# One decoder layer on one core: side work priced by measured durations, the memory norm in pieces, the norm's sums spread out, a final norm from two banks

## The chip, the cores and the metric

The kernel runs on one core of one Trainium2 chip. The metric is the device time of one execution in microseconds, the median of three runs. A core has five engines that matter here: PE (TensorE, matrix products), DVE (VectorE), ACT (ScalarE), POOL (GpSimd) and SP, which only issues transfers. Each engine works through its own queue in order and waits for the others by semaphores. PE writes its results into PSUM banks, from which DVE and ACT read.

## The reference

One layer of a hybrid decoder for a prompt of 256 tokens and 8 sample tokens (264 columns in all), width 2048, in float32:

```python
def layer(x, ...):
    z = rmsnorm(x, g_mix) @ w_in                      # all group inputs from one projection
    # group 1: causal conv, gates, RG-LRU recurrence, gelu, norm   -> y_rg (1024 wide)
    # group 2: mLSTM, 4 heads, key width 128, value width 256
    h_ml, C_new, n_new, m_new = mlstm(q, k, v, logi, logf, C0, n0, m0)
    h_ml = rmsnorm(h_ml, g_ml_out)                    # per head
    y_ml = h_ml * sigmoid(z[..., OFF_O:OFF_I])
    x = x + concatenate([y_rg, y_ml]) @ w_out
    # cross attention: 4 heads over 256 memory tokens; the prompt's keys and values are computed,
    # those of the 8 samples are read from a cache
    x = x + softmax(xq @ mk.T * scale) @ mv @ w_xa_o  # mk, mv = rmsnorm(mem, g_mem) @ w_k, w_v
    xf = rmsnorm(x, g_ffn)
    x = x + (silu(xf @ w_ffn_gate) * (xf @ w_ffn_up)) @ w_ffn_down
# y = rmsnorm(x, g_final)
```

For the 8 sample tokens the mLSTM is one step of the recurrence: C_new = dec * C + k v, num = q . C_new, for each of 4 heads and 8 samples a state of 128 x 256.

## The kernel before, in words

**Weight blocks.** All products with weights are cut into 257 blocks: w_in is blocks 0 to 40, w_out 41 to 56, w_q 57 to 72, w_k and w_v 73 to 104, w_o 105 to 120, the FFN 121 to 256, the last 16 of which are the last part of the down projection. A block gives 128 rows of an output of 264 columns. Its weight of 2048 x 128 comes as two halves (tile `raw`), and each half is split into a high and a low part (tile `W`: high by an ACT copy to fp32r, low by a DVE subtraction). PE computes hi*hi + hi*lo + lo*hi, 48 matmuls of 128x264 a block, 24 a half. `W` has four half buffers, so half k can be written once PE has finished half k-2 blocks. Blocks are counted here in half steps: W of 33.5 is the second half of block 33. The result stands in a PSUM bank `mm`, of which there are four, and is read by an evacuation on DVE (`t<-mm,rstd` or `xres<-xres,mm`). Other products use four banks `ax`.

**Side work** (norms, gates, the mLSTM, attention) is written as Python generators. `side(g, prio)` registers one, and after each block `pump` lets them run, in order of priority, until a price model of DVE and ACT (`price_dve`, `price_act`, `price_pe`, an estimate in us for each instruction) has reached the end of the block by the model of PE; `yield STEP` ends a generator's turn for this block, and a generator of negative priority always runs. `later(f, after=n)` and `drip` put small PE jobs between the weight matmuls, n chunks of them apart. Afterwards a scheduler with a timeline of its own sets the order on each engine; SP's queue is written out by hand. Nearly every instruction passes through one helper, line 63, so in the profile groups are told apart by their tiles.

**The mLSTM's side work** lies in blocks 20 to 40. `ml_prompt` computes for each head h the masked, decayed scores `Pm` (DVE: `B<-ax,gcol`, then two `mask`, then `B<-ax,B 128x384`, with exponentials on ACT between them). `ml_heads` then gives PE the numerators `nps` and the new state `cps` of that head. `ml_sample` works on the sample states: POOL fetches a chunk of four states (`B<-c0T`) and their keys and queries, broadcast to all partitions (`B<-scr`), ACT makes the products k v (`t<-B,B`, two a state), DVE updates the state (`B<-B,bcs,t`, 128x256) and takes its product with q (`t<-B,B` with a sum output that an instruction of its own, DVE_READ_ACCUMULATOR, reads out, two a state). `ml_norm` takes sums of squares over partitions by one-column matmuls with `ones` (`acc_rg` is the like for the other group), makes the norm's factors `f` and spreads them over partitions.

**The memory norm** (`mem_gen`) computes 16 chunks of squares, then their norm, then scales each chunk (POOL, line 998) and splits it into high and low for w_k and w_v.

**The tail.** The squares of the final x are added up in `acc_x`; the sum over partitions is made by one-column matmuls with `ones`, those of the first 15 chunks inside the last block and those of the last chunk behind it (`fin_sums`). `rstd_fin` makes the factor, spreads it (`ax<-ident,c`) and copies it to `rstd` on ACT; DVE multiplies 12 of the 16 chunks of y from the bank, POOL four (chunks 4, 5, 10, 11) from `rstd`, and SP writes `o_y`.

Of the kernel before, what the change touches and what calls it, by code (L numbers as in the profile page):

```python
# [11 lines left out]
F32R = mybir.dt.float32r  # L12
# [5 lines left out]
P = 128  # L18
# [4 lines left out]
N = T + NS  # L23
# [43 lines left out]
def price_dve(name, n, a, k):  # L67
    fast = name in ("tensor_scalar", "tensor_copy", "tensor_single_scalar", "memset")
    if name == "tensor_reduce":
        n = int(np.prod(a[1].shape[1:]))  # L70
    return 0.07 + n * (0.00052 if fast else 0.0066 if name == "reciprocal" else 0.00104)


def price_act(name, n, a, k):
    return 0.12 + n * 0.00083


def price_pe(name, n, a, k):
    passes = 1 if name == "transpose" or a[1].dtype == F32R else 4
    return passes * n * 0.00042 + 0.003  # L80


@with_exitstack
def layer_kernel(ctx: ExitStack, tc, xT, memT, vec, wrg, w_in, w_out, w_q, w_k, w_v, w_o,
# [302 lines left out]
    def rstd_fin(ps):  # L387
        v, r, t = ctile(3), ctile(3), ctile(3)
        dve.tensor_scalar(v, ps[:, :3], 1.0 / D, EPS, op0=OP.mult, op1=OP.add)
        act.activation(r, v, AF.Sqrt)  # L390
        dve.reciprocal(r, r)
        dve.tensor_mul(t, r, r)
        dve.scalar_tensor_tensor(t, t, -0.5, v, op0=OP.mult, op1=OP.mult)
        dve.scalar_tensor_tensor(r, t, 1.5, r, op0=OP.add, op1=OP.mult)
        warm(3, v[:, 0:1])
        ps = bank("ax")
        spread(ps, [r[:, j: j + 1] for j in range(3)])
        act.activation(rstd, ps[:, :N], AF.Copy)
        fin["ps"] = ps

    def fin_sums(ps, x, first):

        for j, w0 in enumerate(WIN):
            pe.matmul(ps[:, j: j + 1], x[:, w0: w0 + P], ones[:, 0:1], start=first and j == 0,
                      stop=not first, skip_group_check=True)

    xres = const.tile([P, KC, N], F32, name="xres")
    acc_x = const.tile([P, N], F32, name="acc_x")
# [313 lines left out]
    def ml_heads():  # L722
        cn = B([P, H, 258])
        hT["t"] = Arr(8)
        hh = hT["t"]
        one = ones[:, 0:1]
        for h in range(H):
            while min(ml.get("pn", 0), ml.get("vtn", 0)) <= h:
                yield STEP
            yield STEP  # L730
            vt = ml["vt", h]
            Pm, kw = ml["w", h]
            nps = bank("ax")
            for vb in range(2):
                o = vb * T
                pe.matmul(nps[:, o: o + T], vt[:, 0, vb * P: vb * P + P], Pm[:, 0:256], start=True, stop=False)
                pe.matmul(nps[:, o + P: o + T], vt[:, 1, vb * P: vb * P + P], Pm[:, 256:384],
                          start=False, stop=True)
            cps = bank("ax")
            pe.matmul(cps[:, 0:258], kw[:, 0:P], vt[:, 0, :], start=True, stop=False)  # L740
            pe.matmul(cps[:, 0:258], kw[:, P:T], vt[:, 1, :], start=False, stop=True)
            dps = cps[:, 300:302]
            pe.matmul(dps[:, 0:1], Pm[:, 0:P], one, start=True, stop=True)
            pe.matmul(dps[:, 1:2], Pm[:, P:T], one, start=True, stop=False)
            pe.matmul(dps[:, 1:2], Pm[:, 256:384], one, start=False, stop=True)
            for vb in range(2):
                act.activation(hh(2 * h + vb)[:, 0:T], nps[:, vb * T: vb * T + T], AF.Copy)
            act.activation(den[:, 3 * h: 3 * h + 2], dps, AF.Abs)
            act.activation(cn[:, h, :], cps[:, 0:258], AF.Copy)
        pool_e.dma_start(o_pc, cn)  # L750
        yield STEP
# [4 lines left out]
    def ml_sample():  # L756
# [42 lines left out]
        for h in range(H):  # L799
            while ml.get("vn", 0) < 2 * h + 2:  # L800
                yield STEP
            for b4 in range(2):
                C, kq = ahead
                n = 2 * h + b4 + 1
                if n < 2 * H:
                    ahead = fetch(n // 2, n % 2)
                for bb in range(4):
                    b = b4 * 4 + bb
                    t2 = tmp(256).rearrange("p (v d) -> p v d", d=P)
                    for vb in range(2):  # L810
                        act.activation(t2[:, vb, :], kq[:, 0, bb, :], AF.Copy,
                                       scale=ml["v"](2 * h + vb)[:, T + b: T + b + 1])
                    dve.scalar_tensor_tensor(C[:, bb], C[:, bb], sc[:, h, b: b + 1], t2, op0=OP.mult, op1=OP.add)
                    j = tmp(P)
                    for vb in range(2):
                        dve.scalar_tensor_tensor(j, C[:, bb, vb, :], 1.0, kq[:, 1, bb, :], op0=OP.mult,
                                                 op1=OP.mult, accum_out=nums[:, 2 * h + vb, b: b + 1])
                    yield 0.8
                pool_e.dma_start(o_sc[h, :, b4 * 4: b4 * 4 + 4], C)
        yield 0.1  # L820

    def ml_norm():
# [26 lines left out]
                dve.tensor_mul(f, f, r)  # L849
            return i  # L850

        k = later(*[lambda h=h: sums(h) for h in range(H)], after=3)
        while k[1]:
            yield STEP
        for h in range(H):
# [101 lines left out]
    def final(m):  # L957

        def f(ps):
            x = xres[:, m, :]  # L960
            if m == 0:
                st["y"] = Arr(KC)
            dve.tensor_add(x, x, ps[:, :N])
            if m < KC - 1:
                sumsq(acc_x, x, m == 0)
            else:
                warm(4)
                sq = tmp()
                with tc.high_priority():
                    act.activation(sq, x, AF.Square)  # L970
                fin_sums(fin["sum"], sq, False)
            act.activation(st["y"](m), x, AF.Copy, scale=V("g_final", m))
            if m == 0:
                act.activation(warm_act, acc_x[:, 0:1], AF.Sqrt)
            elif m == KC - 2:
                fin["sum"] = bank("ax")
                fin_sums(fin["sum"], acc_x, True)
            elif m == KC - 1:
                rstd_fin(fin["sum"])
        return f  # L980

    def mem_gen():
# [5 lines left out]
        acc = ltmp(T)  # L988
        for c in range(KC):
            sumsq(acc, raw(c), c == 0)  # L990
            yield 0.35
        r = ltmp(T)
        yield STEP
        yield from rstd_from(acc, r, D)
        st["mem"] = Side()
        for c in range(KC):
            x = raw(c)
            pool_e.tensor_mul(x, x, r)  # L998
            split(*st["mem"](c), x, V("g_mem", c))
            yield 0.7  # L1000

    def ry(c):
        return st["yrg"](c) if c < 8 else st["yml"](c - 8)
# [360 lines left out]
    for i, (src, cols, pef, evf, need) in enumerate(steps):  # L1364
# [31 lines left out]
        load_piece(i + LD)  # L1396
        pump(pe.clock + SLACK)
        if i == 24:
            ml["ng"] = side(ml_norm(), 6)
        if i == 40:  # L1400
            st["memg"] = side(mem_gen(), 7)
    for e, x in pend:
        e(x)
    for lo, hi in ((0, 1), (1, 2), (2, 4), (4, 6), (6, 8), (8, 10), (10, 12), (12, 14), (14, 16)):
        for c in range(lo, hi):
            e, r = (pool_e, rstd) if c in POOLC else (dve, fin["ps"][:, :N])
            e.tensor_mul(st["y"](c), st["y"](c), r)  # L1407
        sp.dma_start(o_y[:, lo:hi, :], st["y"].tile(lo // 4)[:, lo % 4: lo % 4 + hi - lo, :])
# [106 lines left out]
```

## Time and profile before

| | us |
|---|---|
| median of three runs | 1554.13 (1553.32 to 1554.61) |
| profiled execution, its own time | 1558.61 |
| its span, first to last instruction | 1556.9 |
| PE busy | 1539.4 |
| DVE busy | 1057.4 |
| ACT busy | 782.5 |
| POOL busy | 140.4 |

The mean granted clock of TensorE in that execution is 0.992 of full. In the views below a row of a timeline reads: start and length in us, engine, line, operation, output tile <- input tiles, shape, how many merged into the row, and in brackets the idle time of the engine just before and what it waited for. A length is that of one instruction from its start to its end, so neighbours overlap; what an instruction costs its engine is the distance to the next start. A row of the waits view reads: waiting engine and tile <- engine and tile waited for: us in total, times, longest.

### The profile page before, as it was taken

How to read it: one execution, taken by the hardware profiler on the slowest of the kernel's cores; microseconds unless marked ns; L12 is line 12 of the kernel's file. 1: busy time of each engine (PE TensorE's matmuls, PEld its weight loads, DVE VectorE, ACT ScalarE, POOL GpSimd, SP SyncE). 2: the span in 40 equal slices, each digit the busy share in tenths (PEclk: the TensorE clock that was granted, in tenths of full speed). 3: DMA queues.
4: the chain of work that ended last, by engine and by line, in shares of the span. 5: the costliest groups of instructions: out<-in, count | busy, mean ns of one | idle time of the engine just before them, and what ended most of it. 6: DMA issues, size and time to landing. Idle time of an engine off the chain costs nothing.

```text
span 1556.9 us, 30113 instructions
## 1 busy us (share of the span) xinstructions
PE 1539.4 (99%) x12094; PEld 1505.2 (97%) x12094; DVE 1057.4 (68%) x1984; ACT 782.5 (50%) x1230; POOL 140.4 (9%) x206
## 2 busy tenths in 40 slices
PE   9999999999999999999999999999999999999997
PEld 9999999999999888899999999999999999999997
DVE  7976888787699989876665555455555555555554
ACT  7565765665455566655544444334444433444463
POOL 0001200040134343310000000000000000000000
PEclk9999999999999999999999999999999999999998
DMA  8646785547789887955555555555555555555463
GB/s 298 205 144 216 242 303 190 190 150 243 252 305 349 321 295 252 333 167 177 188 175 181 188 179 188 182 184 186 181 187 180 187 180 188 181 185 181 159 183 104
DMA packets 92172, 326.01 MB, mean 209 GB/s; under 512 B 10784, under 2 KB 11216, under 8 KB 92032
## 3 DMA queue, kind: packets, MB, share of 16 engines
q1 hardware_dynamic: 76608, 270.66, 51.6%
q0 software_dynamic: 15136, 53.16, 9.5%
q8 instruction: 94, 1.54, 0.4%
q14 instruction: 46, 0.38, 0.1%
q10 hardware_dynamic: 288, 0.27, 0.1%
HBM read 312.78 MB, written 11.28 MB: 208 GB/s over the span
## 4 chain that ended last, share of the span: by engine, by line
PE 96%; DVE 2%; DMA 1%; ACT 1%; issue 0%; DVEq 0%; SPq 0%; ACTq 0%; POOLq 0%
PE mm L63 91%; PE ax L63 5%; DVE B L63 1%; DVE W L63 1%; DMA raw<-w_in 1%; DMA B<-scr 0%; DMA scr<-lt 0%; ACT W L63 0%; DMA vecs<-vec 0%; ACT B L63 0%; ACT t L63 0%; ACT L63 0%; DVE t L63 0%; DVE xres L63 0%; DVE acc_x L63 0%
## 5 line engine op out<-in xcount | busy, mean ns | idle before, releaser
L63 PE MATMUL mm<-B,W 128*128 128x264 f32 (+2 forms) x11008 | 1369.2, 285 | 5.1 <-DVE t L63 3.6
L63 PEld LDWEIGHTS mm<-B,W 128*128 128x128 f32 x11008 | 1345.9, 188 | 17.4 <-issue 3.8
L63 DVE TENSOR_TENSOR W<-raw,W 128x1024 fp32r<-128x1024 f32 (+2 forms) x518 | 622.7, 1204 | 361.2 <-ACT W L63 360.0
L63 ACT ACTIVATE W<-raw 128x1024 fp32r<-128x1024 f32 (+2 forms) x518 | 536.4, 1038 | 652.4 <-PE mm L63 455.4
L63 PE MATMUL mm<-W,B 128*128 128x512 f32 x384 | 92.8, 395 | 0.0
L63 PEld LDWEIGHTS mm<-W,B 128*128 128x128 f32 x384 | 70.9, 188 | 16.0
L1407 POOL TENSOR_TENSOR B<-B,rstd 128x264 f32<-128x264 f32 x4 | 2.8, 741 | 855.8 <-ACT rstd L63 855.8
L63 DVE TENSOR_TENSOR t<-mm,rstd 128x264 f32<-128x264 f32 x104 | 44.8, 432 | 45.8 <-PE mm L63 45.4
L63 DVE TENSOR_TENSOR xres<-xres,mm 128x264 f32<-128x264 f32 x80 | 34.2, 427 | 38.1 <-PE mm L63 38.1
L63 DVE SCALAR_TENSOR_TENSOR B<-B,dw 128x256 f32<-128x256 f32 x128 | 55.6, 489 | 4.0 <-ACT dw L63 3.2
L63 PE MATMUL ax<-B,B 128*128 128x256 f32 (+3 forms) x288 | 49.4, 314 | 1.7 <-DVE B L63 1.7
L63 DVE SCALAR_TENSOR_TENSOR dw<-B,qsm,dw 128x256 f32<-128x256 f32 x96 | 49.6, 525 | 0.4
L63 PEld LDWEIGHTS ax<-B,B 128*128 128x128 f32 x288 | 41.4, 193 | 4.6 <-DVE B L63 2.0
L1052 POOL TENSOR_TENSOR dr<-dw,dr 128x256 fp32r<-128x256 f32 x32 | 35.1, 1100 | 107.0 <-ACT dr L63 105.8
L63 ACT ACTIVATE B<-xres,vecs 128x264 fp32r<-128x264 f32 (+1 forms) x64 | 31.2, 504 | 8.2 <-DVE xres L63 5.5
L63 ACT ACTIVATE t<-t 128x264 f32<-128x264 f32 (+1 forms) x61 | 24.8, 407 | 4.0 <-DVE t L63 3.9
L63 ACT ACTIVATE t<-xres 128x264 f32<-128x264 f32 x45 | 18.6, 414 | 15.4 <-DVE xres L63 15.4
L63 ACT ACTIVATE B<-t 128x264 fp32r<-128x264 f32 (+1 forms) x60 | 24.3, 410 | 4.0 <-DVE t L63 3.9
L63 ACT ACTIVATE t<-B,B 128x128 f32<-128x128 f32 x64 | 21.4, 390 | 9.2 <-DMA B<-scr 9.2
L63 DVE SCALAR_TENSOR_TENSOR B<-xres,vecs,B 128x264 fp32r<-128x264 f32 x48 | 23.5, 508 | 3.7 <-ACT B L63 3.7
L63 ACT ACTIVATE dw<-B,qsm 128x256 f32<-128x256 f32 x32 | 16.2, 507 | 17.7 <-DVE B L63 10.7
L998 POOL TENSOR_TENSOR B<-B,lt 128x256 f32<-128x256 f32 x16 | 15.6, 1012 | 94.5 <-ACT lt L63 94.5
(157 smaller groups left out, 673.9 us busy)
## 6 DMA issues: line engine op xcount, KB each, us to landing
raw<-w_gu SPq DMA_DIRECT2D x176, 512.0 KB, 3.5
raw<-w_in SPq DMA_DIRECT2D x80, 512.0 KB, 4.7
raw<-w_d SPq DMA_DIRECT2D x80, 512.0 KB, 3.6
raw<-w_out SPq DMA_DIRECT2D x32, 512.0 KB, 3.7
B<-kcT POOLq DMA_DIRECT2D x32, 512.0 KB, 8.2
raw<-w_q SPq DMA_DIRECT2D x32, 512.0 KB, 5.0
B<-vcT POOLq DMA_DIRECT2D x32, 512.0 KB, 8.7
raw<-w_k SPq DMA_DIRECT2D x32, 512.0 KB, 6.6
```

The lines of the kernel that those rows point to most:

```text
L63: return f(*a, **k)
L998: pool_e.tensor_mul(x, x, r)
L1052: pool_e.tensor_sub(wr[:, 1], acc, wr[:, 0].bitcast(F32))
L1407: e.tensor_mul(st["y"](c), st["y"](c), r)
```

## The change

The price functions get new numbers (sum outputs, scalars from tensors, PE's passes), which changes how much side work each block is handed. `ml_heads` yields one STEP more before each head. `ml_sample` writes its product with q into the first half of `t2` instead of a buffer of its own. `ml_norm` gets negative priority and hands in its four sums as four jobs, one and then three chunks apart. `mem_gen` yields per two sums of squares and after every scaled chunk, and scales on DVE instead of POOL. The final norm takes the last chunk in two halves, sums over partitions once behind the last block, and spreads its factor into two banks, one read by DVE and one by ACT. The output goes out in 6 transfers instead of 9.

```diff
--- before.py
+++ after.py
@@ -68,16 +68,23 @@
     fast = name in ("tensor_scalar", "tensor_copy", "tensor_single_scalar", "memset")
     if name == "tensor_reduce":
         n = int(np.prod(a[1].shape[1:]))
-    return 0.07 + n * (0.00052 if fast else 0.0066 if name == "reciprocal" else 0.00104)
+    p = 0.07 + n * (0.00052 if fast else 0.0066 if name == "reciprocal" else 0.00104)
+    if name == "scalar_tensor_tensor" and not isinstance(a[2], float):
+        p += 0.06
+    return p + (0.12 if "accum_out" in k else 0)
 
 
 def price_act(name, n, a, k):
-    return 0.12 + n * 0.00083
+    p = 0.12 + n * 0.00083
+    if not isinstance(k.get("scale", 1.0), float):
+        p += 0.07
+    return p + (0.2 if "accum_out" in k else 0)
 
 
 def price_pe(name, n, a, k):
-    passes = 1 if name == "transpose" or a[1].dtype == F32R else 4
-    return passes * n * 0.00042 + 0.003
+    if name == "transpose" or a[1].dtype == F32R:
+        return max(0.112, 0.0025 + n * 0.000443)
+    return 2 * max(0.112, n * 0.00085)
 
 
 @with_exitstack
@@ -394,15 +401,12 @@
         dve.scalar_tensor_tensor(r, t, 1.5, r, op0=OP.add, op1=OP.mult)
         warm(3, v[:, 0:1])
         ps = bank("ax")
-        spread(ps, [r[:, j: j + 1] for j in range(3)])
+        cols = [r[:, j: j + 1] for j in range(3)]
+        spread(ps, cols)
+        fin["ps"] = ps
+        ps = bank("ax")
+        spread(ps, cols)
         act.activation(rstd, ps[:, :N], AF.Copy)
-        fin["ps"] = ps
-
-    def fin_sums(ps, x, first):
-
-        for j, w0 in enumerate(WIN):
-            pe.matmul(ps[:, j: j + 1], x[:, w0: w0 + P], ones[:, 0:1], start=first and j == 0,
-                      stop=not first, skip_group_check=True)
 
     xres = const.tile([P, KC, N], F32, name="xres")
     acc_x = const.tile([P, N], F32, name="acc_x")
@@ -728,6 +732,7 @@
             while min(ml.get("pn", 0), ml.get("vtn", 0)) <= h:
                 yield STEP
             yield STEP
+            yield STEP
             vt = ml["vt", h]
             Pm, kw = ml["w", h]
             nps = bank("ax")
@@ -811,9 +816,8 @@
                         act.activation(t2[:, vb, :], kq[:, 0, bb, :], AF.Copy,
                                        scale=ml["v"](2 * h + vb)[:, T + b: T + b + 1])
                     dve.scalar_tensor_tensor(C[:, bb], C[:, bb], sc[:, h, b: b + 1], t2, op0=OP.mult, op1=OP.add)
-                    j = tmp(P)
                     for vb in range(2):
-                        dve.scalar_tensor_tensor(j, C[:, bb, vb, :], 1.0, kq[:, 1, bb, :], op0=OP.mult,
+                        dve.scalar_tensor_tensor(t2[:, 0, :], C[:, bb, vb, :], 1.0, kq[:, 1, bb, :], op0=OP.mult,
                                                  op1=OP.mult, accum_out=nums[:, 2 * h + vb, b: b + 1])
                     yield 0.8
                 pool_e.dma_start(o_sc[h, :, b4 * 4: b4 * 4 + 4], C)
@@ -849,7 +853,8 @@
                 dve.tensor_mul(f, f, r)
             return i
 
-        k = later(*[lambda h=h: sums(h) for h in range(H)], after=3)
+        for h in range(H):
+            k = later(lambda h=h: sums(h), after=3 if h else 1)
         while k[1]:
             yield STEP
         for h in range(H):
@@ -960,23 +965,25 @@
             x = xres[:, m, :]
             if m == 0:
                 st["y"] = Arr(KC)
-            dve.tensor_add(x, x, ps[:, :N])
             if m < KC - 1:
+                dve.tensor_add(x, x, ps[:, :N])
                 sumsq(acc_x, x, m == 0)
             else:
-                warm(4)
+                warm(5)
                 sq = tmp()
                 with tc.high_priority():
-                    act.activation(sq, x, AF.Square)
-                fin_sums(fin["sum"], sq, False)
+                    for lo, hi in ((0, P), (P, N)):
+                        dve.tensor_add(x[:, lo:hi], x[:, lo:hi], ps[:, lo:hi])
+                        act.activation(sq[:, lo:hi], x[:, lo:hi], AF.Square)
+                    for lo, hi in ((0, P), (P, N)):
+                        dve.tensor_add(acc_x[:, lo:hi], acc_x[:, lo:hi], sq[:, lo:hi])
+                sums = bank("ax")
+                token_sums(sums, acc_x)
             act.activation(st["y"](m), x, AF.Copy, scale=V("g_final", m))
             if m == 0:
                 act.activation(warm_act, acc_x[:, 0:1], AF.Sqrt)
-            elif m == KC - 2:
-                fin["sum"] = bank("ax")
-                fin_sums(fin["sum"], acc_x, True)
             elif m == KC - 1:
-                rstd_fin(fin["sum"])
+                rstd_fin(sums)
         return f
 
     def mem_gen():
@@ -988,16 +995,17 @@
         acc = ltmp(T)
         for c in range(KC):
             sumsq(acc, raw(c), c == 0)
-            yield 0.35
+            if c % 2:
+                yield STEP
         r = ltmp(T)
         yield STEP
         yield from rstd_from(acc, r, D)
         st["mem"] = Side()
         for c in range(KC):
             x = raw(c)
-            pool_e.tensor_mul(x, x, r)
+            dve.tensor_mul(x, x, r)
             split(*st["mem"](c), x, V("g_mem", c))
-            yield 0.7
+            yield STEP
 
     def ry(c):
         return st["yrg"](c) if c < 8 else st["yml"](c - 8)
@@ -1396,12 +1404,12 @@
         load_piece(i + LD)
         pump(pe.clock + SLACK)
         if i == 24:
-            ml["ng"] = side(ml_norm(), 6)
+            ml["ng"] = side(ml_norm(), -1)
         if i == 40:
             st["memg"] = side(mem_gen(), 7)
     for e, x in pend:
         e(x)
-    for lo, hi in ((0, 1), (1, 2), (2, 4), (4, 6), (6, 8), (8, 10), (10, 12), (12, 14), (14, 16)):
+    for lo, hi in ((0, 1), (1, 2), (2, 4), (4, 8), (8, 12), (12, 16)):
         for c in range(lo, hi):
             e, r = (pool_e, rstd) if c in POOLC else (dve, fin["ps"][:, :N])
             e.tensor_mul(st["y"](c), st["y"](c), r)
```

By itself the diff does not show which instructions change places. Up to block 23 and after block 109 the orders are alike except for the tail. Three places follow.

DVE, from W of 33 on before: a state update (`B<-B,bcs,t`), dot products (`t,nums<-B,B`), then W of 33.5 (W_2916), and the evacuation of block 28 (`t_2678<-mm_2604`).

```order
L63 TENSOR_TENSOR W_2913<-raw_2828,W_2913 128x8x128
L63 SCALAR_TENSOR_TENSOR B_2545<-B_2545,bcs,t_2664 128x256
L63 SCALAR_TENSOR_TENSOR t_2668,nums<-B_2545,B_2546 128x128 x2
L63 TENSOR_TENSOR W_2916<-raw_2830,W_2916 128x8x128
L63 SCALAR_TENSOR_TENSOR B_2545<-B_2545,bcs,t_2671 128x256
L63 SCALAR_TENSOR_TENSOR t_2675,nums<-B_2545,B_2546 128x128
L63 TENSOR_TENSOR t_2678<-mm_2604,rstd 128x264
```

The same evacuation after (`t_2592<-mm_2499`), behind W of 30 (W_2599):

```order
L63 TENSOR_TENSOR W_2599<-raw_2452,W_2599 128x8x128
L63 TENSOR_TENSOR acc_rg<-acc_rg,t_2490 128x264
L63 SCALAR_TENSOR_TENSOR B_2367<-B_2367,bcs,t_2568 128x256
L63 SCALAR_TENSOR_TENSOR B_2463<-B_2463,bcs,t_2580 128x256
L63 TENSOR_TENSOR t_2592<-mm_2499,rstd 128x264
```

It moved ahead of seven weight halves and the sample work between them.

PE in block 35, the norms' sums before (`acc_rg` for one group, `B_3038` for the four heads of the other):

```order
L63 MATMUL ax_3123<-ones,acc_rg 128x1 x3
L63 MATMUL ax_3143<-ones,B_3038 128x1 x3
L63 MATMUL mm_3153<-B_163,W_3063 128x264
L63 MATMUL mm_3153<-B_164,W_3063 128x264
L63 MATMUL mm_3153<-B_163,W_3063 128x264
L63 MATMUL ax_3143<-ones,B_3038 128x1 x3
```

and after, from the second head's on (`B_3006`):

```order
L63 MATMUL ax_3090<-ones,B_3006 128x1 x3
L63 MATMUL mm_3121<-B_163,W_3031 128x264
L63 MATMUL mm_3121<-B_164,W_3031 128x264
L63 MATMUL mm_3121<-B_163,W_3031 128x264 x2
L63 MATMUL mm_3121<-B_164,W_3031 128x264
L63 MATMUL mm_3121<-B_163,W_3031 128x264
L63 MATMUL mm_3121<-B_173,W_3034 128x264
L63 MATMUL mm_3121<-B_174,W_3034 128x264
L63 MATMUL mm_3121<-B_173,W_3034 128x264 x2
L63 MATMUL mm_3121<-B_174,W_3034 128x264
L63 MATMUL mm_3121<-B_173,W_3034 128x264
L63 MATMUL ax_3090<-ones,B_3006 128x1 x3
```

Between two heads' sums there are now twelve weight matmuls instead of three (six before the first of these).

PE at the end of block 23 before: transposes of a value (`ident,B`), and right behind them head 0's numerators (`ax_2066<-B_1859`, where B_1859 is the Pm of head 0).

```order
L63 MATMUL ax_2060<-ident,B_1876 128x128 x4
L63 MATMUL ax_2066<-B_1859,B_1537 128x256
L63 MATMUL ax_2066<-B_1859,B_1537 128x128
L63 MATMUL ax_2066<-B_1859,B_1537 128x256
L63 MATMUL ax_2066<-B_1859,B_1537 128x128
L63 MATMUL mm_2116<-B_139,W_1986 128x264
```

After, these numerators stand at the end of block 24 and head 0's state `cps` (`ax_2160`) inside block 25:

```order
L63 MATMUL mm_2202<-B_164,W_2081 128x264
L63 MATMUL ax_2160<-B_1537,B_1859 128x258 x2
L63 MATMUL ax_2160<-ones,B_1859 128x1 x3
L63 MATMUL mm_2202<-B_163,W_2081 128x264 x2
L63 MATMUL mm_2202<-B_164,W_2081 128x264
```

The head's work moved one block later on PE. The bank of `ax_2160` is that of `ax_2046`, which DVE reads for head 2's Pm (`B_2049<-ax_2046`); in DVE's new order this stands behind W of 26 (W_2196):

```order
L63 TENSOR_TENSOR W_2196<-raw_2031,W_2196 128x8x128
L63 SCALAR_TENSOR_TENSOR t_2281,nums<-B_2063,B_2064 128x128
L63 SCALAR_TENSOR_TENSOR t_2189,nums<-B_2063,B_2064 128x128
L63 SCALAR_TENSOR_TENSOR t_2269,nums<-B_2063,B_2064 128x128
L63 TENSOR_TENSOR B_2049<-ax_2046,B_2049 128x384
```

So PE's state matmul of head 0 now comes behind four dot products and a weight half that belong to other work.

## The prediction

> **What bounds the kernel now.** I read first the page's engine lines and the chain that ended last, then PE's waits, then a table of stretches with the granted clock, then the timelines around each wait.
>
> ```profile
> PE 1539.4 (99%) x12094; PEld 1505.2 (97%) x12094; DVE 1057.4 (68%) x1984; ACT 782.5 (50%) x1230; POOL 140.4 (9%) x206
> PE 96%; DVE 2%; DMA 1%; ACT 1%; issue 0%; DVEq 0%; SPq 0%; ACTq 0%; POOLq 0%
> L63 PE MATMUL mm<-B,W 128*128 128x264 f32 (+2 forms) x11008 | 1369.2, 285 | 5.1 <-DVE t L63 3.6
> ```
>
> PE carries the chain, and the change leaves its weight matmuls alone: 11008 in 1369.2 us, 0.12 us each, 5.76 for the 48 of a block. So there are only three things to win: idle of PE, matmuls at half clock, and the tail behind the last matmul. PE's waits, longest first:
>
> ```profile
> PE mm L63 <- DVE t L63: 3.6, 1, 3.6
> PE ax L63 <- DVE B L63: 1.7, 1, 1.7
> ...
> PE mm L63 <- DVE W L63: 1.1, 1, 1.1
> ```
>
> Each occurs once. The table of stretches finds them and the half clock (the column behind POOL is the granted clock):
>
> ```profile
> core 0: us, PE busy (x) PEld busy (x) DVE busy (x) ACT busy (x) POOL busy (x), PEclk, DMA share, GB/s
> 159.40:162.80 3.40, 1.68 (x11) 1.25 (x11) 3.40 (x12) 2.27 (x6) 0.54 (x1) 1.00 0.57 200
> 162.80:166.20 3.40, 3.40 (x12) 3.04 (x13) 3.37 (x13) 3.40 (x9) 0.00 (x0) 0.50 0.78 283
> 224.30:227.70 3.40, 0.29 (x2) 0.32 (x3) 2.56 (x9) 1.56 (x4) 0.53 (x1) 1.00 0.57 189
> 227.70:231.10 3.40, 3.40 (x18) 3.40 (x17) 2.54 (x9) 2.25 (x8) 0.00 (x0) 0.50 0.88 265
> 248.10:251.60 3.50, 3.50 (x33) 3.50 (x32) 2.49 (x12) 1.16 (x2) 0.00 (x0) 0.99 0.88 324
> 251.60:258.40 6.80, 6.80 (x33) 6.80 (x32) 3.42 (x15) 1.06 (x1) 0.00 (x0) 0.50 0.39 146
> 347.00:350.60 3.60, 2.54 (x23) 2.33 (x21) 3.60 (x5) 2.62 (x5) 2.44 (x3) 1.00 0.00 0
> 1545.20:1556.90 11.70, 2.47 (x12) 2.37 (x12) 4.82 (x16) 0.43 (x2) 2.85 (x4) 0.50 0.49 185
> ```
>
> After the two long waits the next 3.4 us run at 0.50, and after the stretch at 248 the next 6.8 us do. A stretch at 0.50 does half its work: 1.7, 1.7 and 3.4 us lost. The wait of 1.1 at 349 is followed by no such stretch. The stretch at 248 has no idle; it is thin, because the norm's one-column matmuls stand in it with three weight matmuls between them:
>
> ```profile
> 248.33 0.81 PE L63 MATMUL ax<-ones,B 128*128 128x1 f32 x6
> 249.00 0.61 PE L63 MATMUL mm<-B,W 128*128 128x264 f32 x3
> ```
>
> So 3.6 + 1.7 + 1.1 = 6.4 us of idle and 6.8 us of half clock are there to be won, 13.2 in all.
>
> **The wait at 227 goes: -5.3.** The evacuation that PE waited for stood behind sample work:
>
> ```profile
> 224.96 1.23 DVE L63 TENSOR_TENSOR W<-raw,W 128x1024 fp32r<-128x1024 f32 x1 [0.57 <-ACT W L63]
> 226.10 0.48 DVE L63 SCALAR_TENSOR_TENSOR B<-B,bcs,t 128x256 f32<-128x256 f32 x1
> ...
> 226.83 0.43 DVE L63 TENSOR_TENSOR t<-mm,rstd 128x264 f32<-128x264 f32 x1
> ```
>
> ```profile
> 227.41 2.97 PE L63 MATMUL mm<-B,W 128*128 128x264 f32 x13 [3.58 <-DVE t L63]
> ```
>
> In the new order it stands right behind W of block 30 instead of behind W of 33.5 (blocks counted in half steps), and all evacuations of blocks 25 to 31 stand about two blocks behind their block, with four banks to spare. What covers them: for blocks 28 to 33 DVE gets some 36.7 us of work (1.14 a weight half, 0.40 a state update, 0.22 to 0.33 a dot product, 0.34 an evacuation, by the distances between starts in the rows here and below) against about 40 us of PE. Without that cover an evacuation would be late by the excess; I take none. Both the 3.6 and its 1.7 of half clock go. Bounds: 0 to -5.3; nearest is the whole, since PE runs blocks before and after without waiting.
>
> **The norm sums: -3.4.** The four sums get six or twelve weight matmuls between them where three stood. Six one-column passes take 0.6 to 0.8 us; with twelve full ones of 0.12 behind each six the worst 3.4 us are still about 0.58 full, where the thin stretch had 9 full ones among its 33, 1.1 us of 3.5. The six-pass spreads stay apart too. Bounds -3.4 to 0; I take -3.4, because a stretch with a wait of 1.1, full for 2.54 of 3.60, kept the clock.
>
> **The wait at 161: moved, -0.1 net.** PE waited for head 0's Pm; its matmuls now stand one block later. But the queues that fed it are still late: DVE could start only at 152.59, and up to there the order is the same. What it takes after that:
>
> ```profile
> 152.59 0.48 DVE L63 SCALAR_TENSOR_TENSOR B<-B,bcs,t 128x256 f32<-128x256 f32 x1 [5.43 <-ACT t L63]
> ...
> 156.34 0.29 DVE L63 SCALAR_TENSOR_TENSOR t<-B,B 128x128 f32<-128x128 f32 x1
> ...
> 156.67 0.29 DVE L63 SCALAR_TENSOR_TENSOR t<-B,B 128x128 f32<-128x128 f32 x1
> ...
> 158.18 0.48 DVE L63 SCALAR_TENSOR_TENSOR B<-B,bcs,t 128x256 f32<-128x256 f32 x1
> 158.57 0.43 DVE L63 TENSOR_TENSOR B<-mm,rstd 128x264 f32<-128x264 f32 x1
> 158.91 0.28 DVE L63 SCALAR_TENSOR_TENSOR t<-B,B 128x128 f32<-128x128 f32 x1
> ...
> 159.12 0.74 DVE L63 TENSOR_SCALAR B<-ax,gcol 128x256 f32<-128x256 f32 x2
> ...
> 161.52 0.49 DVE L63 TENSOR_TENSOR B<-B,mask 128x128 f32<-128x128 f32 x2
> ...
> 162.13 0.56 DVE L63 TENSOR_TENSOR B<-ax,B 128x384 f32<-128x384 f32 x1
> ```
>
> and on PE:
>
> ```profile
> 160.42 0.60 PE L63 MATMUL ax<-ident,B 128*128 128x128 f32 x4
> 162.74 2.89 PE L63 MATMUL ax<-B,B 128*128 128x256 f32 x8 [1.72 <-DVE B L63]
> ```
>
> In the new order the next thing that PE meets is head 0's state matmul inside block 25: its bank was last read by head 2's Pm, which stands far down DVE's queue. From 152.59 up to it stand 12 state updates (0.40), 5 weight halves (1.14), 3 Pm (0.47), 3 pairs of masks (0.40), 2 pairs of gcol (0.66), 2 evacuations (0.34) and 22 dot products: 0.21 where the next instruction does not hang on it (158.91 to 159.12), 0.33 behind its own kind (156.34 to 156.67). That is 15.1 us and 4.6 to 7.3: done at 172.3 to 175.0. PE gets there at 160.85 + 5.76 (block 24) + 2.6 (head work at its end) + 2.4 (20 matmuls of 0.12) + 0.7 of two small waits on gcol (0.3 and 0.4) = 172.3. So it waits 0 to 2.7; I take 1.8, nearer the upper end since ACT's exponentials and splits stand in series with these. New idle 2.5 in all, against 1.7 gone. Half clock after it: 0 (like the wait of 1.1) or 1.7 (like the wait of 1.72); 0.8, as this wait can lie across two windows. Net 2.5 + 0.8 - 1.7 - 1.7 = -0.1, between -3.4 and +1.0. [...]
>
> **The memory norm: -1.1.** The 16 products leave POOL for DVE (16 x 0.34 = 5.5 us in one piece behind W of 55.5), and the 16 splits come later in pieces instead of all around 330 to 350. There DVE was slowed to
>
> ```profile
> 348.77 1.76 DVE L63 TENSOR_TENSOR W<-raw,W 128x1024 fp32r<-128x1024 f32 x1
> ```
>
> a weight half, against 1.14 between starts elsewhere, with POOL busy 2.44 of 3.60. The wait at 349 goes. The new bunch: DVE gets to the products when W of 55.5 is written, which its buffer allows about two halves (5.7 us) before PE needs W of 55.5; laid out from there with the prices above, W of 56 is ready some 1.9 us before PE needs it, and behind six splits W of 56.5 0.3 to 1 before (estimates). Bounds -1.1 to +1.5 (six splits late by that much); I take -1.1.
>
> **Prices, reused buffer, one more STEP, memory sums per STEP:** they only reorder; counted above. POOL issues the fetches of sample rows in another order, the first two unchanged, the third earlier. Cost 0.
>
> **The tail: -0.2.**
>
> ```profile
> 1541.79 0.73 PE L63 MATMUL ax<-ones,acc_x 128*128 128x1 f32 x6
> ...
> 1543.97 0.83 PE L63 MATMUL ax<-ones,t 128*128 128x1 f32 x6
> ...
> 1547.70 0.39 ACT L63 ACTIVATE rstd<-ax 128x264 f32<-128x264 f32 x1 [2.47 <-PE ax L63]
> 1548.12 4.16 DVE L63 TENSOR_TENSOR B<-B,ax 128x264 f32<-128x264 f32 x12 [2.09 <-ACT rstd L63]
> 1548.58 4.81 SPq L1408 DMA_DIRECT2D o_y<-B  x9
> ```
>
> The six sum passes leave the last block: -0.56. Two halves plus the add into acc_x instead of one square put the sums about 0.3 later. DVE starts its 12 products right after the first spread, about 0.7 earlier; ACT's rstd and POOL's four products wait for a second spread of six passes (1.3 at half clock), about 1.0 later, so the transfers of chunks 4 to 7 and 8 to 11 go out at about 1550.6 and 1552.0, and the last behind them. Issue to landing and the amount (2.1 MB) do not change, so the end moves -0.9 to +0.6; -0.2.
>
> **Sum:** -5.3 - 3.4 - 0.1 - 1.1 - 0.2 = -10.1. The profiled execution took 1558.61, so 1548.5 by its own time; the median, 4.5 us below it, goes to 1554.13 - 10.1 = 1544.0.
>
> **The rivals.**
> - The heads wait for nothing new: DVE at its lower price, 172.3. Then -3.4 instead of -0.1: 1540.7. For it: most dot products now stand apart. Against: ACT in series.
> - The norm sums stay thin for the gate, as the window's phase falls: 1547.4.
> [...]
> - No change: the late queues carry 7 to 13 us of waits into blocks 25 to 34 in place of those that go: 1554.
> - Slower: ACT's sample products now stand in front of W splits, and they wait for fetched rows,
>
> ```profile
> B<-scr POOLq DMA_DIRECT2D x16, 256.0 KB, 10.0
> ```
>
> ```profile
> ACT t L63 <- DMA B<-scr: 9.2, 3, 6.0
> ```
>
> 10.0 us from issue to landing, and three such waits of up to 6.0. Fetches four to eight are issued only when buffers come free; each us by which such rows are late beyond the 8.6 that three W halves written ahead give (3 x 24 x 0.12) stops PE as long. When that eats the 10.1 and 3.4 more, the kernel is slower: 1557.5. Against it: two of the three waits are short, and PE never waited for one.
>
> **How the numbers follow.** Forecast 0.53 (its own range 1542 to 1546.5), heads free 0.17, norm sums thin 0.10, half clock elsewhere 0.08, no change 0.06, slower 0.06. 0.2% (3.1 us) is about what can be told from no change here: faster 0.88, same 0.06, slower 0.06. The range 1540.0 to 1550.8 leaves out the last two cases and the lower part of the heads' one.
>
> **What would show it.** PE's waits without the evacuation t at 3.6; the clock at 1.00 around the sums of block 35; a wait of ax for DVE's B around 171 of up to 2.7; no wait for W near blocks 51 and 56; the tail's first DVE product right behind the first spread. A wait for W in blocks 25 to 34, or 0.50 in more stretches than one before the tail, would make it wrong.

## The result and the profile after

The changed kernel takes 1545.99 us (median of six, 1545.00 to 1548.01), the kernel before 1554.57 in the same comparison (1553.32 to 1556.30): ratio 0.9946, 95% interval 0.9933 to 0.9958, so -8.4 us, between -10.4 and -6.5. The forecast was 1544.0 within 1540.0 to 1550.8, a fall of 10.1. Ratios leave out one run, of the kernel without the reused buffer below, that took 1888.80 at a mean clock of 0.749 where its ten others had 0.992 to 0.995. The two profiled executions differ by more: 1558.61 before, 1547.03 after, 11.6.

PE's waits in the changed kernel:

```profile
PE ax L63 <- DVE B L63: 1.6, 2, 1.4
PE mm L63 <- DVE ones L63: 1.1, 1, 1.1
PE mm L63 <- DVE c L63: 0.3, 1, 0.3
```

The wait of 3.6 for an evacuation and that of 1.1 for a low half are gone. The one for DVE's B is still there, 1.4 instead of 1.7. The stretches that answer to those of before:

```profile
175.40:178.80 3.40, 3.40 (x17) 3.40 (x17) 1.95 (x5) 1.89 (x4) 2.27 (x5) 0.50 0.84 264
223.00:231.00 8.00, 8.00 (x69) 8.00 (x68) 7.87 (x30) 6.82 (x18) 2.12 (x4) 1.00 0.92 307
241.00:249.00 8.00, 8.00 (x70) 8.00 (x70) 5.93 (x19) 2.78 (x4) 0.00 (x0) 1.00 0.90 348
345.00:352.00 7.00, 7.00 (x61) 7.00 (x60) 4.47 (x10) 3.74 (x5) 0.00 (x0) 1.00 0.49 164
355.00:383.00 28.00, 28.00 (x236) 28.00 (x235) 23.09 (x46) 15.63 (x25) 2.10 (x4) 1.00 0.62 216
```

```profile
360.28 5.46 DVE L63 TENSOR_TENSOR B<-B,lt 128x256 f32<-128x256 f32 x16 [0.31 <-ACT lt L63]
```

PE is busy throughout at a clock of 1.00 where it had waited at 224, where the sums made a thin stretch (now 241 to 249), at 347, and in the blocks around the 16 products of the memory norm, which DVE now makes from 360.28 to 365.7 (355 to 383). One stretch at 0.50 is left before the tail, at 175, behind the new wait. That wait on PE, with DVE's Pm of head 2 that ends it:

```profile
173.22 1.14 PE L63 MATMUL ax<-B,B 128*128 128x258 f32 x4 [1.37 <-DVE B L63]
```

```profile
172.63 0.54 DVE L63 TENSOR_TENSOR B<-ax,B 128x384 f32<-128x384 f32 x1
```

The prediction laid DVE's queue out to end at 172.3 to 175.0, with PE there at 172.3, and took a wait of 1.8; DVE ends at 173.2, PE comes at 171.9, and the wait is 1.4, at the place named. The tail:

```profile
1531.82 0.49 DVE L63 TENSOR_TENSOR xres<-xres,mm 128x128 f32<-128x128 f32 x2 [2.96 <-PE mm L63]
1532.83 0.83 PE L63 MATMUL ax<-ones,acc_x 128*128 128x1 f32 x6
...
1535.82 4.16 DVE L63 TENSOR_TENSOR B<-B,ax 128x264 f32<-128x264 f32 x12 [0.93 <-PE ax L63]
1536.28 4.38 SPq L1416 DMA_DIRECT2D o_y<-B  x6
1536.49 0.39 ACT L63 ACTIVATE rstd<-ax 128x264 f32<-128x264 f32 x1 [2.39 <-PE ax L63]
```

From the first addition of the last chunk to the sums 1.0 us pass (0.9 before), to DVE's first product 4.0 (5.1 before), to ACT's `rstd` 4.7 (4.7 before); the span ends 13.2 us behind that first addition, 13.9 before. The two tails did not run at the same clock: here both spreads ran at 1.00 (12 passes in 1.50 us), while before the half clock began at 1545.2, ahead of the spread.

### The profile page after: what moved, and what is told of

It reads as the page before. It is cut to its first block, busy times and chain, and to the rows that moved or that the text cites. A ratio compares the mean times of both kernels' runs of the same rounds, so it can differ in the third digit from the quotient of the medians.

```text
span 1545.0 us, 30099 instructions
## 1 busy us (share of the span) xinstructions
PE 1533.0 (99%) x12096; PEld 1499.3 (97%) x12096; DVE 1052.7 (68%) x2003; ACT 782.6 (51%) x1231; POOL 124.6 (8%) x190
## 4 chain that ended last, share of the span: by engine, by line
PE 97%; ACT 1%; DMA 1%; DVE 1%; issue 0%; SPq 0%; DVEq 0%; ACTq 0%
PE mm L63 92%; PE ax L63 5%; DVE B L63 0%; DMA xres<-xT 0%; DMA B<-scr 0%; ACT W L63 0%; ACT t L63 0%; ACT B L63 0%; DVE t L63 0%; SPq L1316 0%; ACT L63 0%; DVE c L63 0%; SPq L1309 0%; DVEq L1500 0%; ACT c L63 0%
## 5 line engine op out<-in xcount | busy, mean ns | idle before, releaser
L63 DVE TENSOR_TENSOR xres<-xres,mm 128x264 f32<-128x264 f32 (+1 forms) x81 | 34.3, 424 | 40.4 <-PE mm L63 40.4
L1049 POOL DMA_DIRECT2D B<-kcT x32 | 17.5, 546 | 148.3 <-DVE B L63 138.7
L63 ACT ACTIVATE t<-xres 128x264 f32<-128x264 f32 (+2 forms) x46 | 18.8, 410 | 14.5 <-DVE xres L63 14.5
```

The lines of the kernel that those rows point to most:

```text
L63: return f(*a, **k)
L1049: pool_e.dma_start(kc, kcT[h, b])
```

## The experiments

Two theories stood against each other. Mine: each place has a price of its own, its idle time plus the 3.4 us stretches at half clock behind it. The rival: half clock is not tied to these places, so only idle counts. Beside that, which part of the change did what. The kernel before took 1554.77, 1554.79 and 1555.36 in the three comparisons, its single runs between 1551.6 and 1559.3; that spread is why small differences stay open below. It goes with the clock: of these 60 runs, the five with a mean granted clock of 0.993 took 1557.4 on average, the six with 0.997 took 1552.1.

**One part alone, added to the kernel before.** The final norm:

```diff
...
-                warm(4)
+                warm(5)
...
+                    for lo, hi in ((0, P), (P, N)):
+                        dve.tensor_add(x[:, lo:hi], x[:, lo:hi], ps[:, lo:hi])
+                        act.activation(sq[:, lo:hi], x[:, lo:hi], AF.Square)
...
-    for lo, hi in ((0, 1), (1, 2), (2, 4), (4, 6), (6, 8), (8, 10), (10, 12), (12, 14), (14, 16)):
+    for lo, hi in ((0, 1), (1, 2), (2, 4), (4, 8), (8, 12), (12, 16)):
```

> Before with the new final norm alone. Theory (each place has its own price): the tail term, -0.2 by the prediction, -1.2 by the two profiled tails; so 1554.6 becomes 1553.4 to 1554.4, the three waits of PE and the half clock in blocks 23 to 51 stay. Rival (the tail gained only because the clock window happened to stand well in the one profile of the changed kernel): no change in the median, and its spreads at half clock as before.

1555.23, ratio 1.0001 (0.9989 to 1.0012): between -1.7 and +1.9 us. No gain shown; the theory's lower figure of -1.2 is inside.

The norm's sums:

```diff
-        k = later(*[lambda h=h: sums(h) for h in range(H)], after=3)
+        for h in range(H):
+            k = later(lambda h=h: sums(h), after=3 if h else 1)
...
-            ml["ng"] = side(ml_norm(), 6)
+            ml["ng"] = side(ml_norm(), -1)
```

> Before with ml_norm alone changed (priority -1, four jobs). Theory: no stretch at 0.50 around 250, -3.4 us, 1551.2; PE's three waits stay. Rival (half clock is not tied to thin stretches): the half clock stands there or elsewhere and the time stays within 0.7 us of 1554.6.

1553.08, ratio 0.9992 (0.9983 to 1.0001): -1.2 us, between -2.6 and +0.2. The size of 3.4 is excluded, although the profile has what was expected, no stretch at 0.50 around the sums:

```profile
240.00:256.00 16.00, 16.00 (x137) 16.00 (x137) 12.64 (x38) 8.78 (x16) 0.00 (x0) 1.00 0.71 283
```

Prices, STEP and reused buffer together, and the reused buffer alone (the edit of the second):

```diff
-                    j = tmp(P)
                     for vb in range(2):
-                        dve.scalar_tensor_tensor(j, C[:, bb, vb, :], 1.0, kq[:, 1, bb, :], ...
+                        dve.scalar_tensor_tensor(t2[:, 0, :], C[:, bb, vb, :], 1.0, kq[:, 1, bb, :], ...
```

> Before with the price numbers, the extra STEP and the reused buffer, without the norm, the memory norm and the tail. Theory: PE's wait for the evacuation t (3.6) and its 1.7 of half clock go, the wait at 161 becomes one of 1.4 at 171 with 1.7 of half clock: -5.6, 1549.0; the bunch of sums in block 35 keeps its 3.4 of half clock. Rival (only idle counts): -3.9, 1550.7.

> Before with the reused buffer alone (the product with q goes into t2). Theory: this alone frees buffers t, brings the evacuations of blocks 25 to 31 forward, and takes the wait of 3.6 and its half clock: about -4.5, 1550.2. Rival (the price numbers or the extra STEP did it): the wait t of about 3.6 stays, 1554.7.

Both came to 1549.51 and 0.9965 (0.9953 to 0.9978 and 0.9953 to 0.9977), -5.4 us. PE's waits of the reused buffer alone:

```profile
PE ax L63 <- DVE B L63: 1.4, 1, 1.4
PE mm L63 <- DVE ones L63: 1.1, 1, 1.1
PE mm L63 <- DVE W L63: 1.1, 1, 1.1
```

The wait for t is gone, the one for W (memory norm) stands as before. The evacuation that PE had waited for, the fourth of its kind in this part, started at 226.83 before and starts at 204.51 with the reused buffer alone:

```profile
204.51 0.43 DVE L63 TENSOR_TENSOR t<-mm,rstd 128x264 f32<-128x264 f32 x1
```

The reuse did more than bring evacuations forward: it let instructions that hang on each other be set apart on DVE. Between 145 and 245 us a dot product right behind another starts 0.33 or 0.34 after it in all 20 cases before, 0.20 to 0.22 in 21 of 22 here; right behind a state update it starts 0.51 or 0.52 after it in 25 of 26 cases before, 0.38 to 0.40 in 16 of 18 here. Over those 45 cases that is some 5 us less of DVE time, an estimate, in a stretch of 100 us of which DVE was busy for 77.0 before. Two of the dot products:

```profile
206.04 0.28 DVE L63 SCALAR_TENSOR_TENSOR t<-B,B 128x128 f32<-128x128 f32 x1
206.25 0.08 DVE L63 DVE_READ_ACCUMULATOR t<-B,B 128x1 f32 x1
206.25 0.29 DVE L63 SCALAR_TENSOR_TENSOR t<-B,B 128x128 f32<-128x128 f32 x1
```

How much of the 5.4 comes from the shorter work and how much from the order was not measured. The new price numbers and the STEP show no gain of their own here; each of the two figures is uncertain by about 1.9 either way. The profile with all three has no stretch at 0.50 before the tail, though the bunch of sums, expected to keep its 3.4, and a wait of 1.3 are still in it; that of the reused buffer alone has one, at the bunch.

The memory norm:

```diff
-            yield 0.35
+            if c % 2:
+                yield STEP
...
-            pool_e.tensor_mul(x, x, r)
+            dve.tensor_mul(x, x, r)
             split(*st["mem"](c), x, V("g_mem", c))
-            yield 0.7
+            yield STEP
```

> Before with the memory norm alone changed (per STEP, products on DVE). Theory: the wait of 1.1 for W near 349 goes and none comes: -1.1, 1553.6. Rival (the bunch of 16 products on DVE in block 55 starves W of 56 or 56.5): a wait for W there, no gain.

1553.27, 0.9989 (0.9978 to 1.0000): -1.7, between -3.4 and 0. Its waits:

```profile
PE mm L63 <- DVE t L63: 3.6, 1, 3.6
PE mm L63 <- DVE ones L63: 1.1, 1, 1.1
PE ax L63 <- DVE acc_x L63: 0.7, 1, 0.7
```

None is for W any more; the rival's starving of block 56 did not come.

**The thin stretch measured by itself.** To the changed kernel 30 places were added in the FFN with 30 one-column passes each, results unused, once bunched as block 35 had them before and once set apart:

```diff
+        if 126 <= i < 246 and i % 4 == 2:
+            tb = bank("ax")
+            ts = lambda q, tb=tb: token_sums(tb, rstd, 3 * q)
+            later(lambda: (ts(0), ts(1))[1], lambda: ts(2), lambda: ts(3), lambda: ts(4), after=3)
```

and, set apart, in place of the last line:

```diff
+            later(lambda: ts(0), after=2)
+            for q in range(1, 5):
+                later(lambda q=q: ts(q), after=3 if q > 1 else 1)
```

> The changed kernel with work added: at 30 places in the FFN (every fourth block from 126) the bunch of one-column sums that block 35 had before, 6 + 6, 6, 6, 6 passes with three weight matmuls between (their results are not used). To be compared with the same passes set apart. Theory now: the gate looks at fixed windows of 3.4 us, so a thin stretch of 4.8 us costs none, one or two of them as it falls, about one on average: 1.7 us a place, 51 us more than the spaced one. As the prediction sized it (always two windows): 3.4 a place, 102 us. Rival (thin stretches do not halve the clock): no difference.

> The same 30 places with the same passes, but with 6 to 21 weight matmuls between two sums, as the changed kernel has them in block 35. Theory: 30 x 30 passes of about 0.115 us, 104 us more than the changed kernel (1546.0), so 1650, no stretch at 0.50 in the FFN. Rival (six passes at a time already thin enough): stretches at 0.50 here too.

1700.86 bunched, 1647.42 set apart: 53.4 us for the same passes, 1.78 a place (1.39 to 2.01 by the four single runs of the bunched kernel). A window is here a stretch of 3.4 us at 0.50. Their starts lie on one grid: in the profile of the kernel before the clock falls at 162.82, 227.67, 251.56 and 1545.21, which are 19, 7 and 379 times 3.4133 us apart, in that of the changed kernel at 175.37 and 1540.70, 400 times 3.4133 us apart; the three starts below lie 27.3 us apart, 8 times 3.41. Stretches of the bunched kernel, then the whole FFN part of the other:

```profile
806.20:809.50 3.30, 3.30 (x18) 3.30 (x17) 1.23 (x1) 1.06 (x1) 0.00 (x0) 0.50 0.00 0
833.50:836.80 3.30, 3.30 (x16) 3.30 (x16) 0.99 (x1) 1.06 (x1) 0.00 (x0) 0.50 0.00 0
860.80:867.60 6.80, 6.80 (x34) 6.80 (x33) 1.23 (x1) 1.06 (x1) 0.00 (x0) 0.50 0.19 63
1437.70:1512.70 75.00, 75.00 (x633) 75.00 (x632) 36.47 (x43) 27.22 (x32) 0.00 (x0) 1.00 0.48 161
```

```profile
780.00:1600.00 820.00, 820.00 (x6901) 820.00 (x6900) 396.19 (x484) 301.05 (x359) 0.00 (x0) 1.00 0.48 159
```

The same bunch costs one window (806, 833), two (860), or none (two bunches lie between 1437.7 and 1512.7, at 1.00 throughout). The whole trace has 28 such stretches, 17 of one window and 11 of two, 39 windows in all; the two profiled spans (1705.8 and 1648.0) differ by 57.8, so a window cost about 1.5, not 1.7. Set apart, none of the 30 places has any. So the rival is out, and so is the prediction's figure of two windows each time. The 30 places stand at even distances, so where the windows fall on them is not chance at each, and 1.78 need not be the average over all positions. The place itself bears it out: five profiles of kernels that still have the bunch in block 35 (before, new final norm, new memory norm, reused buffer alone, and with prices and STEP) show 2, 1, 2, 1 and 0 windows there, 1.2 on average.

**Taken from the changed kernel.** First the new wait, by one STEP between head 0's numerators and its state product:

```diff
+            if h == 0:
+                yield STEP
             cps = bank("ax")
```

> The changed kernel with one more STEP between head 0's numerators and its state product, so that the state product stands behind block 25 instead of inside it. Theory: the wait of 1.4 on head 2's Pm goes and with it the one stretch at 0.50 (1.7): 1546.0 becomes 1542.9, and only the tail is at half clock. Rival A (DVE is simply late there): PE waits about as long for the next thing from DVE or ACT, no change. Rival B (half clock comes by itself): -1.4, 1544.6, and a stretch at 0.50 elsewhere.

1544.22, ratio to the kernel before 0.9931 (0.9919 to 0.9943). Its waits, and PE's stretch from block 23 to the tail:

```profile
PE mm L63 <- DVE ones L63: 1.1, 1, 1.1
PE mm L63 <- DVE c L63: 0.3, 1, 0.3
PE mm L63 <- ACT W L63: 0.2, 1, 0.2
PE ax L63 <- DVE B L63: 0.2, 1, 0.2
```

```profile
155.00:1535.00 1380.00, 1378.23 (x10879) 1347.50 (x10878) 929.46 (x1740) 689.26 (x1070) 115.49 (x169) 1.00 0.60 211
```

In this profile the wait is gone and nothing took its place (against rival A), but the median fell by 0.9 to 1.8 (against 1545.12 and 1545.99; by the ratios to the kernel before 1.6 to 2.3), not 3.1, and by the intervals it need not have fallen. It is the fastest version measured.

The changed kernel again, as a reference for the next three:

> The changed kernel once more, beside the next three on the same chip, to compare them with: 1546.0. Its profile falls at another phase of the 3.4 us windows: the wait of about 1.4 on head 2's Pm stays; theory now: 0, 1 or at most 2 windows at 0.50 behind it, no others before the tail. Rival (half clock follows every such wait): exactly one again.

1545.12, 0.9941 (0.9927 to 0.9955). In its profile the wait is shorter, and no stretch at 0.50 follows:

```profile
PE ax L63 <- DVE B L63: 0.6, 1, 0.6
```

```profile
160.00:260.00 100.00, 99.36 (x802) 97.81 (x801) 81.42 (x255) 64.84 (x143) 14.37 (x27) 1.00 0.82 281
```

With the final norm of before:

> The changed kernel with the old final norm. Theory from five profiled tails: last matmul to end 13.2 to 13.9 with the old, 13.2 with the new, and six sum passes (0.56) more inside the last block, so 0.6 to 1.2 slower than the changed kernel: about 1546.9. Prediction's term: 0.2 slower. Rival: no difference.

1545.74, 0.9945 (0.9933 to 0.9958): 0.6 slower, which the intervals do not tell from nothing.

With a buffer of its own for the product with q:

> The changed kernel with a buffer t of its own for the product with q again. Theory: the reused buffer carries the gain of blocks 25 to 34, so the evacuations fall behind again, PE waits for one of them (block 31's, in block 35) by 2 us or more, with half clock behind it: 1549 to 1552. Rival (the price numbers or the STEP carry it): 1546.0.

1554.46, 0.9994 (0.9984 to 1.0005). All but 0.9 us of the gain is lost, more than the 1549 to 1552 expected, and the long wait is not the one expected: PE waits 0.7 for an evacuation, but 3.4 for the input of the norm's sums:

```profile
PE ax L63 <- DVE acc_rg L63: 3.4, 1, 3.4
...
PE mm L63 <- DVE t L63: 0.7, 1, 0.7
```

```profile
238.00:241.90 3.90, 0.56 (x5) 0.35 (x4) 3.68 (x8) 2.59 (x10) 1.68 (x4) 1.00 0.97 278
242.50:259.50 17.00, 17.00 (x80) 17.00 (x80) 7.37 (x32) 4.51 (x7) 0.00 (x0) 0.50 0.44 167
```

The evacuations fall behind again (the dot products are back at 0.32 to 0.34 in 17 of 18 cases, and the evacuation that started at 229.31 in the changed kernel starts at 237.02), the norm's sums in block 35 wait for what DVE makes of them, and then 17 us run at 0.50.

Without the extra STEP:

```diff
             yield STEP
-            yield STEP
             vt = ml["vt", h]
```

> The changed kernel without the extra STEP before each head. Its order has head 0's numerators one block earlier, with a wait like the 1.4, and all 24 one-column passes of the heads' sums in one piece behind block 35. Theory: that piece is thin enough for one window at 0.50 on average: +1.5, 1547.5. Rival (the STEP itself takes the wait at 161 away, worth 3.4): 1549.4. Rival (it does nothing): 1546.0.

1549.87, 0.9965 (0.9952 to 0.9977): 4.7 more than the changed kernel beside it (the intervals overlap by a hair). The theory's 1547.5 was too low; the rival's 1549.4 has the number, but not the whole cause. Its PE rows at both places:

```profile
167.25 4.09 PE L63 MATMUL ax<-B,B 128*128 128x256 f32 x12 [2.40 <-DVE B L63]
```

```profile
249.40 2.74 PE L63 MATMUL ax<-ones,B 128*128 128x1 f32 x24
252.00 0.59 PE L63 MATMUL ax<-ident,c 128*128 128x128 f32 x4
```

```profile
167.60:170.90 3.30, 3.30 (x11) 2.77 (x10) 2.05 (x4) 0.82 (x3) 0.53 (x1) 0.50 0.97 310
252.95:256.30 3.35, 3.35 (x17) 3.35 (x17) 3.27 (x12) 2.08 (x6) 0.00 (x0) 0.50 0.43 150
```

Both causes that were expected apart are there: a longer wait at the heads (2.4) with a window behind it, and 24 one-column passes in one piece with another. This profile is of the slowest of the five runs, 2.0 above their median.

## Why the prediction came out as it did

The direction, the places and the total held. Two terms were wrong in size, in a way that one profile could not show, and one part of the change was wrongly put at nothing. That the fall still came within 1.7 us of the forecast is partly luck: the norm's sums alone gave about 2 less than their term, and the other parts are known no better than to 1.7 to 1.9 either way.

- **The wait at 227, -5.3:** the mechanism is right. The reused buffer alone gives -5.4 (-7.3 to -3.6), and without it the gain is gone. That the size agrees to 0.1 is luck: the wait of 3.6 had one window behind it in three profiles and two in a fourth. What the prediction did not say is that the price numbers, named first in the change, show no part of their own in it; they were never taken out of the whole change by themselves, so a part inside it stays open. Nor did it price the dependent instructions set apart, which the run of the reused buffer alone shows.
- **The norm's sums, -3.4:** the step that failed is "the worst 3.4 us are still about 0.58 full, where the thin stretch had 9 full ones among its 33", priced at the two windows of the profile. The mechanism held (set apart: no window in 30 places), but the bunch costs none to two windows as it falls, 1.78 us on average in the 30 places, and -1.2 (-2.6 to +0.2) was measured alone.
- **The wait at 161, -0.1 net:** the new wait was foreseen to 0.4 us (1.4 for 1.8) and is 0.6 and 1.4 in two profiles of the changed kernel. What went was smaller than the profile's 1.7. Three kernels have the order of before here; PE's rows at that place in the ones with the final norm and the norm's sums:

```profile
162.53 1.57 PE L63 MATMUL ax<-B,B 128*128 128x256 f32 x8 [0.29 <-DVE B L63]
```

```profile
162.61 1.58 PE L63 MATMUL ax<-B,B 128*128 128x256 f32 x8 [1.08 <-DVE B L63]
```

  In the third, with the memory norm, no such wait is listed. It hangs on when the first fetched rows land beside PE's own progress, and varies from 0 to 1.7: in these three and the kernel before, ACT's first product on the rows starts at 151.65, 151.74, 150.89 and 151.87, head 0's Pm on DVE 10.26 or 10.27 us behind it each time, and PE comes by between 161.0 and 162.2. One of the four has a window behind the wait.

  Of the new order there are five profiles: four waits for head 2's Pm of 1.37, 0.64, 0.87 and 0.99, and in the fifth (the sums set apart), where the rows landed 2.5 to 3.2 us later, a wait of 1.65 at 162.75; two of the five, 1.37 and 1.65, have a window behind them. No run shows the 0.8 of half clock that the sum took for a wait across two windows; two windows of 1.7 in five profiles are 0.7 on average. By these averages the term is a loss of about half a microsecond, an estimate.

  The prediction's bounds for it do not follow from its own parts either: 0 to 2.7 of wait, 0.7 of small waits and 0 to 1.7 of half clock against 3.4 gone give -2.7 to +1.7, not -3.4 to +1.0, and the rival at 1540.7 should have stood at 1541.4. Of the 0.7 of small waits the changed kernel's profile shows 0.2.
- **The memory norm, -1.1:** it fits: -1.7 (-3.4 to 0), the wait for W gone, none in block 56.
- **The tail, -0.2:** not settled: +0.2 (-1.7 to +1.9) alone, 0.6 between the changed kernel with and without it. The profiles show DVE's first product 1.1 earlier behind the last chunk's addition, where 0.7 had been worked out, and ACT's `rstd` no later, where 1.0 had been; but one of the two tails had its spread at half clock and the other had not.
- **"They only reorder; cost 0" for the STEP:** wrong inside the whole change, where leaving it out costs about 4.7, though with the prices it shows no gain over the reused buffer alone. By the profile without it, the STEP keeps the heads' work away from late queues and, with the norm's jobs of negative priority, keeps their sums from coming in one piece; how the 4.7 divides between the two was not measured.
- **The sum:** the parts alone give -5.4 - 1.2 - 1.7 + 0.2 = -8.1, the whole -8.4 and -9.2. With 1.4 to 1.9 of uncertainty on each part this agreement does not show that the parts simply add up, and the runs without the buffer and without the STEP show that they do not. The profile's own 11.6 compares an execution with four windows before the tail and 6.4 us of the waits named with one that has one window and 1.6; the first is 4.0 above the median of its kernel, the second 1.0. The mean clock of that first execution, 0.992, lies below all 60 runs of the same kernel in the three comparisons (0.993 to 0.997). Applying its terms to the median was the general fault. The term of the norm's sums lies about midway between the forecast's -3.4 and the 0 of the rival at 1547.4.

## What to carry to other kernels

A stall or half-clock stretch seen in one profile is one draw: here the wait at 161 was 0 to 1.7 us in four profiles, as the fetched rows landed, and the same bunch of sums had none, one or two windows of 3.4 us at it. Before pricing such a place, look in more than one profile at what it hangs on, and price it at its average. Six small matmuls between twelve large ones brought no window in 30 places here; with three large ones between them they cost 1.78 us a place more. Side work shared a small rotating buffer with the evacuations, and freeing one buffer (-5.4 us alone) did more here than the new prices of the planner, which showed no gain of their own; with it, instructions that hang on each other no longer had to stand next to each other (0.20 to 0.22 us between the starts of two dot products where it had been 0.33 or 0.34).

## What the runs showed of the hardware

Half clock lasted in one kernel. Sums of six passes with twelve weight matmuls between had no window in 30 places (1.00 from 780 to 1600), but in the kernel without the reused buffer, behind a wait of 3.4 us, the same pattern stood at half clock for five windows, 17 us at 0.50, until plain weight matmuls followed (1.00 from 259.6 to 270). The same twelve and six, at 0.50 in that kernel and at 1.00 in the changed one:

```profile
243.99 2.99 PE L63 MATMUL mm<-B,W 128*128 128x264 f32 x12
246.77 1.27 PE L63 MATMUL ax<-ones,B 128*128 128x1 f32 x6
247.91 2.99 PE L63 MATMUL mm<-B,W 128*128 128x264 f32 x12
```

```profile
244.70 1.68 PE L63 MATMUL mm<-B,W 128*128 128x264 f32 x12
246.22 0.72 PE L63 MATMUL ax<-ones,B 128*128 128x1 f32 x6
246.81 1.69 PE L63 MATMUL mm<-B,W 128*128 128x264 f32 x12
```

By the distances between starts (3.92 and 2.11 us for twelve and six) a window's length of 3.4 us held about 10 weight matmuls at 0.50 and about 19 at 1.00, an estimate. In the kernel before, counting those that reach over an edge, the 3.4 us of the bunch ahead of the half clock (248.15 to 251.56) had 9; of the two windows at 0.50 behind it the first had 12 and another at 0.50 followed, the second 17 and 1.00 followed. At which count the clock falls, at which it comes back, and whether these are the same, was not shown. From 242.5 to 259.5 PE was busy all the time (17.00 of 17.00 us) and still at 0.50, so PE's busy time in a profile does not tell its clock.
